# State-space set-up recast: paired complex products, blockwise powers, work moved to ScalarE and GpSimd

## The chip, the cores and the metric

The kernel runs on one core of one Trainium2 chip. The metric is the device time of one execution in microseconds (us); of the kernel before there are three timed runs, and the median counts.

## The reference, cut to what matters

One trunk layer is applied to two sequences of 1024 tokens (D_MODEL 1024) with the same weights: RMSNorm, one input projection, four token mixers (RG-LRU, gated linear attention, gated DeltaNet, S5), a gated merge, an output projection, a final norm. Two pieces matter here. DeltaNet's q, k and v go through a depthwise convolution of four taps and SiLU:

```python
qkv = jax.nn.silu(centred_dwconv(qkv.astype(f32), conv_w.astype(f32)))
```

S5 is a diagonal complex recurrence in 32 groups of 64 states, forward and reverse. Its parameters are made discrete from the weights alone:

```python
dt = jnp.exp(log_dt)[:, None]
mag = jnp.exp(lam_re * dt)
a_re, a_im = mag * jnp.cos(lam_im * dt), mag * jnp.sin(lam_im * dt)
...
bb_re = f_re[..., None] * b_re - f_im[..., None] * b_im
bb_im = f_re[..., None] * b_im + f_im[..., None] * b_re
...
s[t] = a * s[t-1] + bb @ u[t]        # complex, per group
y[t] = c_re @ s_re[t] - c_im @ s_im[t]
```

Nothing of the S5 set-up depends on the sequence.

## The kernel before, in words

The two sequences run one after the other (`for s in range(nseq)`), each in stages. A stage opens its own memory and PSUM banks and hands its generators to `weave`, which draws a step from whichever generator is least far along; this gives the order of the program. A framework scheduler with a simulated timeline then fixes the order of instructions on each engine, so work of a generator can move a little ahead or behind its place in the program. Engines run their own list in order. All operations go through small helpers, so the profile names line 54 for nearly all of them, and groups are told apart by tile names.

The stages of a sequence are, in order:

- **Projection stage.** `dn_proj` makes q, k, v and a gate for four heads, 16 steps. Each is one projection of 1024 x 128 in three-pass fp32r (`proj_steps`, 48 matmuls of 512 columns, weights split into `hi` on ScalarE and `lo` on GpSimd), evicted by ScalarE into `dup`. For q, k, v the convolution follows: one `tensor_scalar` for the first tap and three `scalar_tensor_tensor` for the others, all on VectorE (`conv`, tile `dcv`), then a sigmoid on ScalarE (`dsg`), a product on GpSimd, and, one step later, transposes on TensorE. Beside it run some blocks of the merge gate's projection (`early`, two of 48 matmuls in the first sequence, none in the second), and in the first sequence alone `s5_setup`, with 8 steps.
- **Recurrence stage.** `dn_core1` (triangular inverses of DeltaNet) and the RG-LRU blocks; in the first sequence also `s5_rot`, which builds a table of rotations for each of eight quads of groups and stores it (`rot_d`).
- **Attention and S5 stage**, then the merge and output stages. `s5_core` loads the stored tables.

`s5_setup` computes on 128 partitions (64 states x two directions). From small tiles of 128 x 32 (`s5t`) it makes the powers of a from 0 to 8 (`pw`), the rotations' seven squarings (`rot`), bb (`s5bb`), c transposed (`s5cc`) and re-ordered powers (`s5pwo`, 64 copies). Then each of eight quads of four groups forms two complex outer products on VectorE (`M` with `tq` as scratch, real and imaginary part each as two products and a sum), stores one (`tout_d`), transposes the other on TensorE (`Ti`, `tin_d`), copies the first shifted into `s5CA`, and multiplies bb with `s5CA` on TensorE into a bank where group g takes output partitions 32g to 32g+15; ScalarE evicts that into `Kt`, VectorE adds a diagonal (`dm`), and eight stores follow (`tk_d`). The matmul of that last step is:

```python
for ri in range(2):
    for g in range(4):
        mm(p[g * 32:g * 32 + 16, 0:240], bb[:, ri, qd * 4 + g],
           CA[:, ri, g].rearrange("p l i -> p (l i)"), start=(ri == 0), stop=(ri == 1))
```

All loads and stores of DRAM are issued by SyncE's queue in order.

## Time and profile before

| | |
|---|---|
| timed runs | 3162.29, 3163.14, 3171.67 us; median 3163.14 us |
| profiled execution, its own time | 3163.6 us |
| its span, first to last instruction | 3161.9 us (1.7 us around it) |
| mean granted TensorE clock | 0.961 of full speed |
| TensorE matmul, busy | 2884.7 us (91%), 15130 instructions |
| VectorE, busy | 1970.0 us (62%), 3909 instructions |
| ScalarE, busy | 1247.2 us (39%) |
| GpSimd, busy | 1075.7 us (34%) |

Busy time is the union of an engine's instructions, so overlapping matmuls are counted once. An average over the span mixes stages; the rows below therefore come from single stretches. A tile's row lists the instructions that read or write it. "Releaser" is what ended an engine's wait as the semaphores show it.

### The profile page before, as it was taken

How to read it: one execution, taken by the hardware profiler on the slowest of the kernel's cores; microseconds unless marked ns; L12 is line 12 of the kernel's file. 1: busy time of each engine (PE TensorE's matmuls, PEld its weight loads, DVE VectorE, ACT ScalarE, POOL GpSimd, SP SyncE). 2: the span in 40 equal slices, each digit the busy share in tenths (PEclk: the TensorE clock that was granted, in tenths of full speed). 3: DMA queues.
4: the chain of work that ended last, by engine and by line, in shares of the span. 5: the costliest groups of instructions: out<-in, count | busy, mean ns of one | idle time of the engine just before them, and what ended most of it. 6: DMA issues, size and time to landing. Idle time of an engine off the chain costs nothing. (4 is left out here: it accounts for less than half of the span.)

```text
span 3161.9 us, 41900 instructions
## 1 busy us (share of the span) xinstructions
PE 2884.7 (91%) x15130; PEld 2367.2 (75%) x15130; DVE 1970.0 (62%) x3909; ACT 1247.2 (39%) x1926; POOL 1075.7 (34%) x851
## 2 busy tenths in 40 slices
PE   6888779999996999999999988999999699999998
PEld 5666667778785788878778866777878588788877
DVE  6999786733658455665655367673366744557645
ACT  4333545543223334332354355653332334333223
POOL 2267552432343222111343333343324222221123
PEclk9999989999998999999999998999999899999999
DMA  5344535242242445563453342434224244565343
GB/s 105 98 125 149 177 102 159 80 150 67 87 142 89 142 138 185 195 203 121 162 186 103 102 135 83 154 89 138 67 90 142 86 142 127 188 207 193 117 150 124
DMA packets 430449, 418.97 MB, mean 133 GB/s; under 512 B 109953, under 2 KB 323489, under 8 KB 430241
## 3 DMA queue, kind: packets, MB, share of 16 engines
q1 hardware_dynamic: 430240, 416.29, 42.2%
q8 instruction: 119, 1.95, 0.3%
q14 instruction: 90, 0.73, 0.1%
HBM read 302.68 MB, written 113.51 MB: 132 GB/s over the span
## 5 line engine op out<-in xcount | busy, mean ns | idle before, releaser
L54 PE MATMUL pj<-xn,hi 128*128 128x512 f32 x4608 | 1481.0, 401 | 18.9 <-DVE misc L54 4.4
L54 POOL TENSOR_TENSOR lo<-raw,hi 128x512 fp32r<-128x512 f32 x432 | 614.0, 1425 | 1441.3 <-ACT hi L54 1333.2
L54 PEld LDWEIGHTS pj<-xn,hi 128*128 128x128 f32 x4608 | 871.6, 192 | 213.4 <-issue 11.7
L54 PE MATMUL pj<-xn,lo 128*128 128x512 f32 x2304 | 918.0, 398 | 0.0
L54 ACT CAST hi<-raw 128x512 fp32r<-128x512 f32 x432 | 265.1, 618 | 732.8 <-PE pj L54 498.7
L54 PEld LDWEIGHTS pj<-xn,lo 128*128 128x128 f32 x2304 | 441.9, 192 | 101.0 <-issue 7.9
L54 ACT ACT_TABLE_LOAD x194 | 248.9, 1283 | 140.6 <-DVE Ab L54 81.6
L54 PE MATMUL pj<-yh,hi 128*128 128x512 f32 x576 | 237.4, 412 | 3.2 <-DVE mg L54 3.2
L54 PE MATMUL pj<-yh,lo 128*128 128x512 f32 x576 | 226.1, 393 | 0.0
L54 PE MATMUL pj<-yl,hi 128*128 128x512 f32 x576 | 225.7, 392 | 0.2 <-DVE yl L54 0.2
L54 DVE TENSOR_TENSOR sg<-sg,pj 128x512 f32<-128x512 f32 x128 | 87.6, 685 | 97.3 <-PE pj L54 82.2
L54 PE MATMUL pj<-hi,mh 128*128 128x512 f32 x384 | 124.6, 401 | 6.4 <-ACT mh L54 4.1
L54 PEld LDWEIGHTS pj<-yh,lo 128*128 128x128 f32 x576 | 108.7, 189 | 23.8
L54 PEld LDWEIGHTS pj<-yh,hi 128*128 128x128 f32 x576 | 109.1, 189 | 22.3 <-DVE mg L54 4.0
L54 PEld LDWEIGHTS pj<-yl,hi 128*128 128x128 f32 x576 | 109.3, 190 | 18.9 <-DVE yl L54 0.5
L54 DVE TENSOR_TENSOR_SCAN w<-E,v 64x512 f32<-64x512 f32 x64 | 97.6, 1525 | 18.8 <-PE s L54 17.9
L54 ACT ACTIVATE fg<-pj,bmg 128x512 f32<-128x512 f32 x112 | 76.7, 686 | 69.8 <-issue 30.4
L54 DVE TENSOR_TENSOR yl<-yr,yh 128x512 fp32r<-128x512 f32 x80 | 59.5, 751 | 66.9 <-ACT yh L54 66.7
L54 POOL TENSOR_TENSOR v<-E,w 128x512 f32<-128x512 f32 x32 | 57.4, 1794 | 122.3 <-issue 71.2
L54 ACT ACTIVATE vn<-r,beta 128x128 f32<-128x128 f32 x128 | 40.5, 364 | 147.9 <-DVE vs L54 139.9
L54 DVE SCALAR_TENSOR_TENSOR dcv<-dup,dn_cw,dcv 128x1024 f32<-128x1024 f32 x72 | 96.8, 1344 | 1.3
L54 DVE TENSOR_TENSOR mg<-mg,sg 128x512 f32<-128x512 f32 x96 | 94.9, 989 | 2.1
(375 smaller groups left out, 4553.5 us busy)
## 6 DMA issues: line engine op xcount, KB each, us to landing
raw<-in_w_in_dram SPq DMA_DIRECT2D x176, 256.0 KB, 2.9
raw<-in_w_merge_gate_dram SPq DMA_DIRECT2D x128, 256.0 KB, 3.2
sl<-rows_d SPq DMA_DIRECT2D x128, 256.0 KB, 6.7
gs_d<-fg SPq DMA_DIRECT2D x112, 256.0 KB, 2.6
sg<-gs_d SPq DMA_DIRECT2D x112, 256.0 KB, 2.9
sl<-qkv_d SPq DMA_DIRECT2D x40, 512.0 KB, 4.6
raw<-in_w_branch_dram SPq DMA_DIRECT2D x64, 256.0 KB, 3.3
yr<-ysp SPq DMA_DIRECT2D x64, 256.0 KB, 3.2
```

The costliest lines, as they stand in the source:

```text
L54: i = f(*a, **kw)
```

## The change

It concerns the set-up of S5, and the first convolution tap of the first sequence.

- `conv` gets an argument: in the first sequence the first tap of DeltaNet's convolution is a scaled Copy on ScalarE instead of a VectorE `tensor_scalar` (12 of 1024 elements per partition). The second sequence keeps VectorE.
- Powers of a are made in three blocks (2; 3 and 4; 5 to 8) instead of seven steps, and a square takes 4 VectorE operations instead of 7.
- `s5bb` and `s5cc` each get a second, rotated copy (made on ScalarE), and `s5pwo` holds each power twice (16 ScalarE copies instead of 64 on VectorE). So each complex outer product is two products and one sum of 1024 elements per partition, instead of six operations of 512 and one sign change.
- `s5CA` and its copies are gone. The matmuls into `Kt` read `M` itself: per group three column ranges (112, 16 and 112 columns), each with its own weights (`b2` is bb with the other direction's half zero), real and imaginary part accumulated. The groups are now the outer loop. The diagonal is added by GpSimd.
- `s5_rot` does real and imaginary part in one operation, all of a quad on VectorE for even quads and on GpSimd for odd ones.
- `s5_setup` yields 32 times (8 while it loads c, 24 in the quads) instead of 8.

```diff
-    def conv(out, up, cw, bias=None):
-        if bias is None:
+    def conv(out, up, cw, bias=None, first=None):
+        if first is S:
+            act(out, up[:, 0:T], AF.Copy, scale=cw[:, 0:1])
+        elif bias is None:
             ts(V, out, up[:, 0:T], cw[:, 0:1], None, ALU.mult)
         else:
             ts(V, out, up[:, 0:T], cw[:, 0:1], bias, ALU.mult, ALU.add)
...
-            conv(cv, up, dn_cw[:, i * 4 + h])
+            conv(cv, up, dn_cw[:, i * 4 + h], first=S if s == 0 else V)
...
-    def cmul(ore, oim, are, aim, bre, bim, ta, tb, eng=V):
-        tt(eng, ta, are, bre, ALU.mult)
-        tt(eng, tb, aim, bim, ALU.mult)
-        tt(eng, tb, ta, tb, ALU.subtract)
-        tt(eng, ta, are, bim, ALU.mult)
-        tt(eng, oim, aim, bre, ALU.mult)
-        tt(eng, oim, oim, ta, ALU.add)
-        eng.tensor_copy(ore, tb)
+    def cmul(ore, oim, are, aim, bre, bim, ta, tb):
+
+        tt(V, ta, are, bre, ALU.mult)
+        tt(V, tb, aim, bim, ALU.mult)
+        tt(V, ore, ta, tb, ALU.subtract)
+        tt(V, ta, are, bim, ALU.mult)
+        tt(V, tb, aim, bre, ALU.mult)
+        tt(V, oim, ta, tb, ALU.add)
+
+    def csquare(ore, oim, re, im, ta, tb):
+        tt(V, ta, re, re, ALU.mult)
+        tt(V, tb, im, im, ALU.mult)
+        stt(oim, re, 2.0, im, ALU.mult, ALU.mult)
+        tt(V, ore, ta, tb, ALU.subtract)
...
+            eng = V if qd % 2 == 0 else G
...
-            for lv in range(7):
+            V.tensor_copy(E[:, 0:2, :, 1], rot[:, 0:3:2, 0, gs])
+            for lv in range(1, 7):
                 m = 1 << lv
-                b0, b1 = bc(rot[:, 0, lv, gs], m), bc(rot[:, 1, lv, gs], m)
-                e0, e1 = E[:, 0, :, 0:m], E[:, 1, :, 0:m]
-                f0, f1 = E[:, 0, :, m:2 * m], E[:, 1, :, m:2 * m]
-                tv = pl.tile([128, 4, 64], F32, tag="tm", name=nm("tm"))[:, :, 0:m]
-                tv2 = pl.tile([128, 4, 64], F32, tag="tm2", name=nm("tm2"))[:, :, 0:m]
...
-                tt(V, f0, e0, b0, ALU.mult)
-                tt(V, tv, e1, b1, ALU.mult)
-                tt(V, f0, f0, tv, ALU.subtract)
-                tt(G, f1, e0, b1, ALU.mult)
-                tt(G, tv2, e1, b0, ALU.mult)
-                tt(G, f1, f1, tv2, ALU.add)
+                both = [128, 2, 4, m]
+                e, f = E[:, 0:2, :, 0:m], E[:, 0:2, :, m:2 * m]
+                y = E[:, 2].rearrange("p a n -> p (a n)")[:, 0:8 * m].rearrange("p (r a n) -> p r a n", r=2, a=4)
+                tt(eng, f, e, bc(rot[:, 0, lv, gs].unsqueeze(1).to_broadcast([128, 2, 4]), m), ALU.mult)
+                tt(eng, y, e[:, ::-1], bc(rot[:, 1:3, lv, gs], m), ALU.mult)
+                tt(eng, f, f, y, ALU.add)
...
-        for e in range(2, 9):
-            cmul(pw[:, 0, e], pw[:, 1, e], pw[:, 0, e - 1], pw[:, 1, e - 1], pw[:, 0, 1], pw[:, 1, 1], ta, tb)
+        for e in (1, 2, 4):
+            n_ = [128, e, 32]
+            pa, pb = (pl.tile([128, 4, 32], F32, tag=x, name=nm(x))[:, 0:e] for x in ("pa", "pb"))
+            top = [pw[:, i, e].unsqueeze(1).to_broadcast(n_) for i in range(2)]
+            cmul(pw[:, 0, e + 1:2 * e + 1], pw[:, 1, e + 1:2 * e + 1], pw[:, 0, 1:e + 1], pw[:, 1, 1:e + 1], *top, pa, pb)
...
-        ts(V, tb[64:128], tb[64:128], -1.0, None, ALU.mult)
+        ts(V, sn[64:128], sn[64:128], -1.0, None, ALU.mult)
         tc_, td = t32(), t32()
-        for _ in range(3):
-            cmul(ta, tb, ta, tb, ta, tb, tc_, td)
-        V.tensor_copy(rr[:, 0], ta)
-        V.tensor_copy(ri[:, 0], tb)
+        csquare(tc_, td, cs, sn, ta, tb)
+        csquare(cs, sn, tc_, td, ta, tb)
+        csquare(rot[:, 0, 0], rot[:, 2, 0], cs, sn, ta, tb)
         for e in range(1, 7):
-            cmul(rr[:, e], ri[:, e], rr[:, e - 1], ri[:, e - 1], rr[:, e - 1], ri[:, e - 1], ta, tb)
+            csquare(rot[:, 0, e], rot[:, 2, e], rot[:, 0, e - 1], rot[:, 2, e - 1], ta, tb)
+        ts(V, rot[:, 1, 0:7], rot[:, 2, 0:7], -1.0, None, ALU.mult)
...
-            bb = ep.tile([128, 2, 32, 16], F32, name="s5bb")
-            braw = ep.tile([128, 2, 32, 16], F32, name="s5braw")
+
+            bb = ep.tile([128, 2, 32, 2, 16], F32, name="s5bb")
+            spare = ep.tile([128, 2, 2, 32, 16], F32, tag="b2", name="s5braw")
+            braw, tq = spare[:, 0], spare[:, 1, 0]
...
-                tt(V, bb[:, o], braw[:, x0], bc(fre, 16), ALU.mult)
+                b_ = bb[:, 0, :, o]
+                tt(V, b_, braw[:, x0], bc(fre, 16), ALU.mult)
                 tt(V, tq, braw[:, x1], bc(fim, 16), ALU.mult)
-                tt(V, bb[:, o], bb[:, o], tq, op)
-            cc = ep.tile([128, 2, 32, 16], F32, name="s5cc")
+                tt(V, b_, b_, tq, op)
+            act(bb[:, 1, :, 0], bb[:, 0, :, 1], AF.Copy, scale=-1.0)
+            S.copy(bb[:, 1, :, 1], bb[:, 0, :, 0])
+            cc = ep.tile([128, 2, 32, 2, 16], F32, name="s5cc")
             for i, nme in enumerate(("s5_c_re", "s5_c_im")):
...
+                    yield
                     transpose(p[:, b * 128:(b + 1) * 128], ld.rearrange("x d p -> x (d p)"), ident)
-                V.tensor_copy(cc[:, i].rearrange("p g i -> p (g i)"), p)
-
-            pwo = ep.tile([128, 2, 2, 32, 8], F32, name="s5pwo")
+                p3 = p.rearrange("p (g i) -> p g i", i=16)
+                if i == 0:
+                    S.copy(cc[:, 0, :, 0], p3)
+                    act(cc[:, 1, :, 1], p3, AF.Copy, scale=-1.0)
+                else:
+                    act(cc[:, 0, :, 1], p3, AF.Copy, scale=-1.0)
+                    S.copy(cc[:, 1, :, 0], cc[:, 0, :, 1])
+
+            b2 = ep.tile([128, 2, 32, 2, 16], F32, tag="b2", name="s5b2")
+            G.memset(b2, 0.0)
+            for d in range(2):
+                S.copy(b2[d * 64:d * 64 + 64, d], bb[d * 64:d * 64 + 64, 0])
+
+            pwo = ep.tile([128, 2, 2, 32, 2, 8], F32, name="s5pwo")
             for ri in range(2):
-                for t_ in range(8):
-                    V.tensor_copy(pwo[0:64, 0, ri, :, t_], pw[0:64, ri, 7 - t_])
-                    V.tensor_copy(pwo[64:128, 0, ri, :, t_], pw[64:128, ri, t_])
-                    V.tensor_copy(pwo[0:64, 1, ri, :, t_], pw[0:64, ri, t_ + 1])
-                    V.tensor_copy(pwo[64:128, 1, ri, :, t_], pw[64:128, ri, 8 - t_])
...
-            CA = ep.tile([128, 2, 4, 15, 16], F32, name="s5CA")
-            V.memset(CA, 0.0)
             for qd in range(NQ):
                 gs = slice(qd * 4, qd * 4 + 4)
                 prod = {}
-                for io, src in ((0, bb), (1, cc)):
-                    sh = [128, 4, 8, 16] if io else [128, 4, 16, 8]
-                    M = ep.tile(sh[:2] + [2] + sh[2:], F32, tag=f"M{io}", name=nm("M"))
-                    tq4 = ep.tile(sh, F32, tag=f"tq{io}", name=nm("tq4"))
-                    eng = V
-                    if io:
-                        P_ = lambda ri: bc(pwo[:, 1, ri, gs], 16)
-                        B_ = lambda ri: src[:, ri, gs].unsqueeze(2).to_broadcast(sh)
-                    else:
-                        P_ = lambda ri: pwo[:, 0, ri, gs].unsqueeze(2).to_broadcast(sh)
...
-                    tt(eng, M[:, :, 0], P_(0), B_(0), ALU.mult)
-                    tt(eng, tq4, P_(1), B_(1), ALU.mult)
-                    tt(eng, M[:, :, 0], M[:, :, 0], tq4, ALU.subtract)
-                    tt(eng, M[:, :, 1], P_(0), B_(1), ALU.mult)
-                    tt(eng, tq4, P_(1), B_(0), ALU.mult)
-                    tt(eng, M[:, :, 1], M[:, :, 1], tq4, ALU.add)
-                    if io == 1:
-                        ts(eng, M[:, :, 1], M[:, :, 1], -1.0, None, ALU.mult)
-                    prod[io] = M
+                for io, src in ((1, cc), (0, bb)):
+                    sh = [128, 8, 8, 16] if io else [128, 8, 16, 8]
+                    M = ep.tile(sh, F32, tag=f"M{io}", name=nm("M"))
+                    Y = ep.tile(sh, F32, tag="Y", name=nm("Y"))
+                    for o, i in ((M, 0), (Y, 1)):
+                        P_ = pwo[:, io, i, gs].rearrange("p g r t -> p (g r) t")
+                        B_ = src[:, i, gs].rearrange("p g r i -> p (g r) i")
+                        if io:
+                            P_, B_ = bc(P_, 16), B_.unsqueeze(2).to_broadcast(sh)
+                        else:
+                            P_, B_ = P_.unsqueeze(2).to_broadcast(sh), bc(B_, 8)
+                        tt(V, o, P_, B_, ALU.mult)
+                    tt(V, M, M, Y, ALU.add)
+                    prod[io] = M.rearrange("p (g r) a b -> p g r (a b)", r=2)
                 Mi, Mo = prod[0], prod[1]
-                dma(tout_d[qd], Mo.rearrange("p g r t i -> p g r (t i)"))
+                dma(tout_d[qd], Mo)
+                yield
...
-                        transpose(p[:, g * 128:(g + 1) * 128],
-                                     Mi[:, g, ri].rearrange("p j t -> p (j t)"), ident)
+                        transpose(p[:, g * 128:(g + 1) * 128], Mi[:, g, ri], ident)
...
-                for ri in range(2):
-                    V.tensor_copy(CA[0:64, ri, :, 8:15], Mo[0:64, :, ri, 0:7])
-                    V.tensor_copy(CA[64:128, ri, :, 0:7], Mo[64:128, :, ri, 1:8])
-                    ts(V, CA[:, ri, :, 7], cc[:, ri, gs], 1.0 if ri == 0 else -1.0, None, ALU.mult)
                 Kt = ep.tile([16, 4, 240], F32, tag="Kt", name=nm("Kt"))
+                yield
                 p = bank("st")
-                for ri in range(2):
-                    for g in range(4):
-                        mm(p[g * 32:g * 32 + 16, 0:240], bb[:, ri, qd * 4 + g],
-                           CA[:, ri, g].rearrange("p l i -> p (l i)"), start=(ri == 0), stop=(ri == 1))
+                for g in range(4):
+                    gg = qd * 4 + g
+                    for o, w, x in ((slice(0, 112), b2[:, 1], lambda ri: Mo[:, g, ri, 16:128]),
+                                    (slice(112, 128), bb[:, 0], lambda ri: cc[:, 0, gg, ri]),
+                                    (slice(128, 240), b2[:, 0], lambda ri: Mo[:, g, ri, 0:112])):
+                        for ri in range(2):
+                            mm(p[g * 32:g * 32 + 16, o], w[:, gg, ri], x(ri), start=(ri == 0), stop=(ri == 1))
...
-                tt(V, dm, ident[0:16, 0:16].unsqueeze(1).to_broadcast([16, 4, 16]), bc(dT[:, gs], 16), ALU.mult)
-                tt(V, Kt[:, :, 112:128], Kt[:, :, 112:128], dm, ALU.add)
+                tt(G, dm, ident[0:16, 0:16].unsqueeze(1).to_broadcast([16, 4, 16]), bc(dT[:, gs], 16), ALU.mult)
+                tt(G, Kt[:, :, 112:128], Kt[:, :, 112:128], dm, ALU.add)
...
-                    rot = bp.tile([128, 2, 8, 32], F32, name="rot")
-                    todo.append((8, s5_setup(pool("s5s", 1, stack=st), rot)))
+                    rot = bp.tile([128, 3, 8, 32], F32, name="rot")
+                    todo.append((32, s5_setup(pool("s5s", 1, stack=st), rot)))
```

## Rows read from the trace of the kernel before

**Rows 1.** Engines by stretch: PE, PEld, DVE, ACT, POOL busy us (count), PEclk, DMA, GB/s
```profile
49.30:337.80 288.50, 244.98 (x1174) 187.28 (x1175) 275.47 (x688) 109.42 (x186) 155.90 (x155) 0.95 0.38 122
1658.90:1846.70 187.80, 184.00 (x850) 149.02 (x849) 89.00 (x141) 83.80 (x126) 70.07 (x44) 1.00 0.33 101
337.80:743.30 405.50, 356.80 (x1933) 286.53 (x1932) 247.11 (x464) 201.65 (x278) 166.33 (x163) 0.94 0.41 125
1846.70:2240.70 394.00, 354.64 (x1910) 284.97 (x1910) 231.08 (x398) 199.49 (x273) 139.47 (x98) 0.93 0.39 118
```
**Rows 2.** First sequence, tiles that mark the projection stage's two ends: duration min/median/max, starts
```profile
L54 ACT COPY dup<-pj x24: 569/585/592, 49.3 to 312.7; 128x512 f32<-128x512 f32 x24
L529 SPq DMA_DIRECT2D rows_d<-rs x1: 737/737/737, 337.8 to 337.8; - x1
```
**Rows 3.** VectorE groups by shape, 60 to 340 us: busy us, mean ns | idle before
```profile
L54 DVE TENSOR_TENSOR M<-s5pwo,s5cc 128x512 f32<-128x512 f32 x16 | 19.6, 1252 | 0.0
L54 DVE COPY s5pwo<-pw 64x32 f32<-64x32 f32 x60 | 13.3, 226 | 0.7
L54 DVE TENSOR_TENSOR M<-s5pwo,s5bb 128x512 f32<-128x512 f32 x16 | 13.1, 840 | 0.0
L54 DVE TENSOR_SCALAR dcv<-dup,dn_cw 128x1024 f32<-128x1024 f32 x12 | 12.9, 1072 | 0.9 <-ACT dup L54 0.8
L54 DVE TENSOR_TENSOR s5t<-pw 128x32 f32<-128x32 f32 x21 | 7.2, 364 | 0.1
L54 DVE TENSOR_SCALAR M<-M 128x512 f32<-128x512 f32 x8 | 4.4, 548 | 0.0
```
**Rows 4.** Stretch, busy of tiles tq, dm, then E (DVE, POOL), E again (recurrence stage)
```profile
49.30:337.80 288.50, 49.93 (x64) 0.95 0.38 122
...
49.30:337.80 288.50, 7.35 (x15) 0.95 0.38 122
...
49.30:337.80 288.50, 32.18 (x108) 69.89 (x105) 0.95 0.38 122
...
337.80:743.30 405.50, 16.84 (x66) 28.11 (x63) 0.94 0.41 125
```
**Rows 5.** The same for tile s5CA: PE, PEld and DVE
```profile
49.30:337.80 288.50, 9.00 (x128) 2.47 (x128) 24.29 (x48) 0.95 0.38 122
```
**Rows 6.** Prices: VectorE product of 1024, ScalarE scaled pass of 1024, a weight load
```profile
L54 DVE TENSOR_TENSOR i<-i,r x16: 1201/1226/1803, 390.2 to 2151.8; 128x1024 f32<-128x1024 f32 x16
...
L54 ACT ACTIVATE a<-r,sp8n x16: 1147/1152/1157, 377.0 to 2139.8; 128x1024 f32<-128x1024 f32 x16
...
L54 PEld LDWEIGHTS st<-s5CA,s5bb x128: 92/95/97, 137.9 to 317.6; 128*16 128x16 f32 x128
```
**Rows 7.** Timeline of TensorE: start us, us, operation, count
```profile
203.16 0.60 PE L54 MATMUL st<-s5CA,s5bb 128*16 128x240 f32 x8 [1.44 <-DVE s5CA L54]
203.69 0.74 PE L54 MATMUL pj<-xn,hi 128*128 128x512 f32 x2
...
207.02 0.62 PE L54 MATMUL pj<-xn,hi 128*128 128x512 f32 x2
207.48 0.39 PE L54 MATMUL pj<-xn,lo 128*128 128x512 f32 x1
...
209.30 0.60 PE L54 MATMUL st<-ident,M 128*128 128x128 f32 x4
209.66 0.48 PE L54 MATMUL pj<-xn,hi 128*128 128x512 f32 x1
```
**Rows 8.** Timeline of GpSimd and VectorE over one collision
```profile
194.40 2.95 POOL L54 TENSOR_TENSOR dcv<-dcv,dsg 128x1024 f32<-128x1024 f32 x1
195.01 2.41 DVE L54 TENSOR_TENSOR dm<-ident,s5dT 16x64 f32<-16x64 f32 x1
```
**Rows 9.** Waits: us in total, times, longest; 40 to 335 us, then 330 to 480 us
```profile
ACT hi L54 <- DMA raw<-in_w_in_dram: 32.1, 7, 9.8
...
DVE E L54 <- DMA rot_d<-E: 7.7, 1, 7.7
```

More of the change, by code (lines that the diff above doesn't have):

```diff
@@ L1120, in s5_setup @@
                     dma(braw[d * 64:(d + 1) * 64, i], A[nme][0, d].rearrange("g p j -> p g j"))
-            tq = ep.tile([128, 32, 16], F32, name="s5tq")
             for o, (x0, x1, op) in ((0, (0, 1, ALU.subtract)), (1, (1, 0, ALU.add))):
-                tt(V, bb[:, o], braw[:, x0], bc(fre, 16), ALU.mult)
+                b_ = bb[:, 0, :, o]
+                tt(V, b_, braw[:, x0], bc(fre, 16), ALU.mult)
                 tt(V, tq, braw[:, x1], bc(fim, 16), ALU.mult)
-                tt(V, bb[:, o], bb[:, o], tq, op)
-            cc = ep.tile([128, 2, 32, 16], F32, name="s5cc")
+                tt(V, b_, b_, tq, op)
+            act(bb[:, 1, :, 0], bb[:, 0, :, 1], AF.Copy, scale=-1.0)
+            S.copy(bb[:, 1, :, 1], bb[:, 0, :, 0])
+            cc = ep.tile([128, 2, 32, 2, 16], F32, name="s5cc")
             for i, nme in enumerate(("s5_c_re", "s5_c_im")):
@@ L1132, in s5_setup @@
                         dma(ld[:, d], A[nme][0, d, b * 8:(b + 1) * 8].rearrange("g i p -> (g i) p"))
+                    yield
                     transpose(p[:, b * 128:(b + 1) * 128], ld.rearrange("x d p -> x (d p)"), ident)
-                V.tensor_copy(cc[:, i].rearrange("p g i -> p (g i)"), p)
-            pwo = ep.tile([128, 2, 2, 32, 8], F32, name="s5pwo")
-            for ri in range(2):
-                for t_ in range(8):
-                    V.tensor_copy(pwo[0:64, 0, ri, :, t_], pw[0:64, ri, 7 - t_])
-                    V.tensor_copy(pwo[64:128, 0, ri, :, t_], pw[64:128, ri, t_])
-                    V.tensor_copy(pwo[0:64, 1, ri, :, t_], pw[0:64, ri, t_ + 1])
-                    V.tensor_copy(pwo[64:128, 1, ri, :, t_], pw[64:128, ri, 8 - t_])
+                p3 = p.rearrange("p (g i) -> p g i", i=16)
[10 more added lines that the diff above has]
+            pwo = ep.tile([128, 2, 2, 32, 2, 8], F32, name="s5pwo")
+            for ri in range(2):
+                w = pw[:, ri].rearrange("p e g -> p g e")
+                for x in range(2):
+                    S.copy(pwo[0:64, 0, ri, :, x], w[0:64, :, 7::-1])
+                    S.copy(pwo[64:128, 0, ri, :, x], w[64:128, :, 0:8])
+                    S.copy(pwo[0:64, 1, ri, :, x], w[0:64, :, 1:9])
+                    S.copy(pwo[64:128, 1, ri, :, x], w[64:128, :, 8:0:-1])
             dT = ep.tile([16, 32], F32, name="s5dT")
             dma(dT, A["s5_d"][0].rearrange("(g j) -> j g", j=16))
-            CA = ep.tile([128, 2, 4, 15, 16], F32, name="s5CA")
-            V.memset(CA, 0.0)
             for qd in range(NQ):
@@ L1175, in s5_setup @@
                     for g in range(4):
-                        transpose(p[:, g * 128:(g + 1) * 128],
-                                     Mi[:, g, ri].rearrange("p j t -> p (j t)"), ident)
+                        transpose(p[:, g * 128:(g + 1) * 128], Mi[:, g, ri], ident)
                     S.copy(Ti[:, :, ri], p.rearrange("p (g n) -> p g n", g=4))
                 dma(tin_d[qd], Ti)
-                for ri in range(2):
-                    V.tensor_copy(CA[0:64, ri, :, 8:15], Mo[0:64, :, ri, 0:7])
-                    V.tensor_copy(CA[64:128, ri, :, 0:7], Mo[64:128, :, ri, 1:8])
-                    ts(V, CA[:, ri, :, 7], cc[:, ri, gs], 1.0 if ri == 0 else -1.0, None, ALU.mult)
                 Kt = ep.tile([16, 4, 240], F32, tag="Kt", name=nm("Kt"))
+                yield
                 p = bank("st")
-                for ri in range(2):
-                    for g in range(4):
-                        mm(p[g * 32:g * 32 + 16, 0:240], bb[:, ri, qd * 4 + g],
-                           CA[:, ri, g].rearrange("p l i -> p (l i)"), start=(ri == 0), stop=(ri == 1))
+                for g in range(4):
[5 more added lines that the diff above has]
+                            mm(p[g * 32:g * 32 + 16, o], w[:, gg, ri], x(ri), start=(ri == 0), stop=(ri == 1))
                 for g in range(4):
```

7 lines of the change are left out of this document (removed).

## The prediction, made from the kernel before alone

> **What bounds the kernel now.** The change touches the first sequence only, so I first looked for the same stage in both sequences and laid one beside the other, in the view of busy time by stretch. The stage's ends are read from two tiles: the first eviction of a projection into the convolution's input at 49.3 us and the store of the decay rows at 337.8 us [rows 2]; the second sequence's marks are the same instructions. In the first sequence the projection stage lasts 288.5 us, in the second 187.8 us [rows 1]. In the second TensorE is busy for 184.0 of 187.8 us at the full clock (2.4 GHz): it is the bound. In the first it is busy for 245.0 of 288.5 us at a mean of 0.95 of the clock, and it is VectorE that hardly pauses: 275.5 of 288.5 us, against 89.0 in the second sequence [rows 1]. The difference, 186.5 us, is the S5 set-up that runs beside. So in this one stage VectorE is the bound, and time taken from it comes back until TensorE's own work is the limit.
>
> How far away is that limit? A projection's matmul of 512 columns follows the one before it after 0.23 us (two in 0.46 us) [rows 7]. The stage holds everything that the second sequence's has (187.8 us), two more blocks of 48 matmuls (96 x 0.23 = 22.1 us), the transposes of the outer products (16 batches of four, 0.36 us from one batch's start to the next matmul, 5.8 us), some four such batches for c (1.4 us), and the matmuls into the convolution kernel: eight instructions per batch, 0.53 us to the next matmul [rows 7], 128 instructions [rows 5], so 16 batches, 8.5 us. That is 225.6 us of TensorE work in 288.5 us: 62.9 us are lost to waits and to the lower clock that goes with them.
>
> The recurrence stage offers nothing: it takes 405.5 us in the first sequence and 394.0 in the second [rows 1]; the first has one more block of the merge gate (48 x 0.23 = 11.0 us), which is all of the difference. The rotation tables that are built there cost no time now.
>
> **VectorE, part by part.** What leaves it altogether: the shifted copies, 24.3 us [rows 5]; the re-ordered powers, 13.3; the first tap, 12.9; the sign change, 4.4 [rows 3]; the diagonal, 7.4 [rows 4]. Sum 62.3 us. The outer products: the scratch tile's instructions are 49.9 us [rows 4] and the first products into M 19.6 and 13.1 [rows 3], together 82.6 us for 96 operations of 512. Afterwards there are 48 of 1024. At the price of an undisturbed product of that size, 1.226 us [rows 6], they cost 58.8 us; if each costs as much as the two it replaces, 82.6. I take the middle, 71: what stretches these instructions (their means are up to 1.25 us [rows 3]) is seen where GpSimd holds one: a VectorE sum of 64 elements takes 2.41 us and ends with GpSimd's product [rows 8]; and half as many can be held. Saved 12, between 0 and 24. Powers and squarings: 7 steps of 7 become 3 of 6, and 9 of 7 become 9 of 4, so 58 small operations fewer; at 0.226 to 0.364 us [rows 3] 13 to 21 us, and I take 15. The rotation tables: VectorE's part is 32.2 us in this stage and 16.8 in the next [rows 4], 49 for eight quads. It now does four quads with as many operations as before, each twice as long, so between 24 and 49 us, in either stage. In this stage it may lose 32 or gain 17; I take a gain of 9. VectorE is then left with 275.5 - 62.3 - 12 - 15 - 9 = 177 us, at least 135 and at most 217.
>
> **TensorE.** Its work grows. The new matmuls into Kt have 112, 16 and 112 columns, so as many columns as before, but the loop order is turned. Before, four groups stood one behind the other, each writing another strip of 32 output partitions, and the timeline shows what that gives: eight matmuls of 240 columns are over in 0.60 us [rows 7], where 512 columns of the same data type need as much to their end, so the strips work side by side. Now twelve instructions of one strip follow each other. Nothing in the trace shows small matmuls of one strip in a row; I bound them. Below: they overlap as today, 8.5 us. Above: the columns one after the other. There are 64 products, two passes each (128 records [rows 5]), of 240 columns, 30,720 columns. The transposes have the same data type: 512 columns take 0.36 us to the next matmul and 0.60 us to their end [rows 7], 0.70 or 1.17 ns a column, so 21.6 or 36 us. I take 24, near the step to the next matmul, since the matmuls behind don't wait for the last one's end. TensorE's work becomes 225.6 - 8.5 + 24 = 241 us. That is above VectorE's highest bound, so TensorE sets the stage.
>
> On top come waits. With none, as in the second sequence, the stage lasts 241 us; with all that are there now, 304, which would be a loss. I take 14 us, far nearer to the second sequence, since the same code without a full VectorE loses 3.8 us there; what is added is that the front of the stage still has a chain of small operations ahead of its first quad and that TensorE now meets transposes that wait for M. So 255 us, a gain of 33.5 us.
>
> **ScalarE, GpSimd, SyncE.** ScalarE takes 12 taps at 1.15 us [rows 6] = 13.8 us and 24 copies of at most 1024 elements, at most 27.6 us: at most 151 of 255 us with the 109.4 it has [rows 1]. The tap stands at the head of a chain that it leads on the same engine anyway (evict, tap, three VectorE taps, sigmoid), so it costs nothing as long as ScalarE isn't held; behind it are queued the next casts of weights. GpSimd loses the shared levels (69.9 us in this stage [rows 4]) and gets four whole quads, 56 to 112 us in either stage (14 us a quad now, twice the length then), and 16 small sums: at most 216 of 255. The number of DMAs is unchanged, and SyncE's queue carries the same stores; those of the last quad move from an eighth before the stage's end to its end, where eight stores stand ahead of the decay rows. I cost that at nothing, since the next stage opens with projections that need none of them; without that cover it costs a few microseconds, which the 14 us hold.
>
> The profiled execution took 3163.6 us, against a median of 3163.1, so the same sum holds for both: 3163.6 - 33.5 = 3130 us.
>
> **Rivals.** (1) The strips overlap after all, or waits vanish: the stage lasts 226 to 230 us, 3103 us. Against it: only the order of issue changed, and a strip has one set of weights at a time.
>
> (2) Weight loads come into the open. Each of the 384 new matmuls brings its own load of 95 ns [rows 6], as long as a matmul of 112 columns streams (79 ns). If none is hidden, 36.5 us more: 241 + 36.5 + 14 = 292 us, 3167 us, no change. Against it: eight such loads are issued with eight matmuls within 0.60 us, and the projections' loads hide behind 0.23 us [rows 7]. The Trainium skill, TensorE: Matmul & The Clock Gate, Part 3, says that a weight load overlaps matmuls in flight only where the row group differs; these all use the same rows, so by that rule this rival would be the case. The trace disagrees for the projections, whose loads use all rows too and hide; the same page lets a load into a background buffer go ahead.
>
> (3) The tap on ScalarE is held behind weight casts that wait for SyncE's loads: seven such waits, 32.1 us, up to 9.8 us each [rows 9]. If all of them pass on through the convolution to the transposes, the gain is gone: 3162 us. Against it: the sigmoid stands behind the same casts in the second sequence, and TensorE is full there.
>
> (4) Slower: the rotation table has one buffer. VectorE clears it for every quad and then must wait for GpSimd's whole quad and its store. Such a wait is there once now, 7.7 us [rows 9]. Behind it stand, in VectorE's order, the convolutions and evictions of either stage. Four GpSimd quads of 14 us give 56 us; if it all reached the path, 3130 + 56 = 3186 us. It decides from 43 us on. Against it: VectorE is idle for 158 us of the recurrence stage [rows 1], and the order is fixed with GpSimd's time in view.
>
> (5) VectorE stays the bound because GpSimd stretches it more than today; it would have to exceed its upper bound by a fifth. Then about 3140 to 3150 us.
>
> **How the numbers follow.** The forecast, with 3112 to 3150 around it, gets 0.68; (1) 0.05; (2) 0.08; (3) 0.08; (4) 0.08; (5) 0.03. About 0.3% (9.5 us) is what a measurement can tell from no change. Faster: 0.68 + 0.05 + 0.03 = 0.76; within: (2) and (3), 0.16; slower: (4), 0.08. The range runs from 3106, below which lies most of (1), to 3163, above which lie (4) and half of (2).
>
> **What would show it.** After the change the first sequence's projection stage should last about 255 us with TensorE busy in over 90% of it and VectorE in 150 to 200 us; a batch into Kt should take some 3 us per quad instead of two of 0.53; the recurrence stage should stay at 405 us within 5. Wrong would be: a stage of 280 us and more with VectorE idle; VectorE waits on the rotation table of tens of microseconds; a recurrence stage that is longer.

## The result, and the profile after

The changed kernel takes 3131.6 us (median of four, 3128.1 to 3137.0), the kernel before, timed beside it, 3162.7 us: a ratio of 0.9893 with a 95% interval of 0.9871 to 0.9915, so 31 us less; 3130 had been forecast. The profiled execution of the changed kernel takes 3133.5 us.

The busy time by stretch, first sequence, cut at the same marks as before: the projection stage, the recurrence stage, and the same two stretches for tile E (the rotation tables) alone. Columns as in [rows 1].

```profile
49.50:302.00 252.50, 240.62 (x1367) 194.38 (x1367) 170.63 (x292) 135.15 (x215) 101.65 (x65) 0.97 0.39 123
302.00:709.20 407.20, 364.02 (x1998) 292.29 (x1994) 262.25 (x497) 204.08 (x284) 190.68 (x197) 0.95 0.43 134
...
49.50:302.00 252.50, 0.00 (x0) 0.00 (x0) 0.97 0.39 123
302.00:709.20 407.20, 33.55 (x96) 54.10 (x96) 0.95 0.43 134
```

Beside [rows 1]: the projection stage is 36.0 us shorter (288.5 to 252.5); VectorE is busy for 171 of 252 us instead of 275 of 288, TensorE for 95% of the stage instead of 85%. The recurrence stage is 1.7 us longer, its start 0.2 us later, and everything behind it, whose code is the same, 4.0 us longer (2418.6 to 2422.6; over all profiles of this study this part lies between 2408 and 2423 us, so that is scatter). -36.0 + 1.7 + 0.2 + 4.0 = -30.1 us, the difference of the two profiled executions.

The last two lines show what was not forecast: against [rows 4], no rotation table at all is built in the projection stage now. Both engines do all of it in the recurrence stage. A table begins with two short operations on VectorE that set its first entries. The row of these operations, in the kernel before and then in the changed one (count, duration ns, first and last start us), and what the first one waits for in the changed kernel:

```profile
L54 DVE MEMSET E<- x16: 62/62/62, 3.8 to 431.0; 128x4 f32 x16
L54 DVE MEMSET E<- x16: 62/62/62, 311.3 to 515.3; 128x4 f32 x16
DVE E L54 <- DMA tk_d<-Kt: 8.0, 1, 8.0
```

In the kernel before the first table is begun at 3.8 us. In the changed one it is begun at 311.3 us, after a wait of 8.0 us for the last store of the last quad's `Kt`. Nothing in the arithmetic ties a table to `Kt`; in the program, memory that one pool gives back is taken by a later one, tile by tile (`reuse_waits`). So the tables now seem to lie in memory that the set-up uses to its end. That the set-up's new tile sizes moved them there is likely, and not shown.

VectorE's and ScalarE's groups in the projection stage of the changed kernel (busy us, mean ns | idle before, releaser), the new ones:

```profile
L54 DVE TENSOR_TENSOR M<-M,Y 128x1024 f32<-128x1024 f32 x16 | 26.9, 1684 | 0.4
L54 DVE TENSOR_TENSOR Y<-s5pwo,s5cc 128x1024 f32<-128x1024 f32 x8 | 13.8, 1726 | 0.2
L54 DVE TENSOR_TENSOR Y<-s5pwo,s5bb 128x1024 f32<-128x1024 f32 x8 | 13.1, 1634 | 0.2
L54 DVE TENSOR_TENSOR M<-s5pwo,s5cc 128x1024 f32<-128x1024 f32 x8 | 11.2, 1400 | 35.6 <-PE st L54 18.3 <-ACT s5cc L54 17.3
L54 DVE TENSOR_TENSOR M<-s5pwo,s5bb 128x1024 f32<-128x1024 f32 x8 | 10.5, 1318 | 18.2 <-PE st L54 18.2
...
L54 ACT COPY s5pwo<-pw 64x256 f32<-64x256 f32 x16 | 10.5, 658 | 3.3 <-DVE pw L54 3.1
```

The five product groups sum to 75.5 us (71 forecast). VectorE now waits: for TensorE's work that frees M (18.3 us for the matmuls into Kt, which read one product, and 18.2 us for the transposes of the other), and once for the transposed c (17.3 us, until ScalarE's copy `s5cc`). That copy follows the last transpose of c, which TensorE runs at 128.8 us in its order and without a pause before it; the loads for it were issued by 120.0 us and land 1.6 to 3.9 us later. In the kernel before, M's products hardly waited [rows 3]: the wait has changed sides.

TensorE's waits in the stage (us in total, times, longest), changed kernel:

```profile
PE pj L54 <- DVE dtk L54: 5.3, 1, 5.3
PE sm L54 <- DVE rw L54: 3.3, 1, 3.3
PE cr L54 <- DVE GG L54: 2.9, 1, 2.9
PE cr L54 <- DVE g L54: 0.4, 1, 0.4
```

That is 11.9 us, all of TensorE's idle time (252.5 - 240.6); before it was idle for 43.5.

The matmuls into Kt, TensorE's timeline over one batch (start us, us, operation):

```profile
186.33 0.61 PE L54 MATMUL pj<-xn,hi 128*128 128x512 f32 x2
186.88 0.56 PE L54 MATMUL st<-M,s5b 128*16 128x112 f32 x4
187.27 0.25 PE L54 MATMUL st<-s5cc,s5bb 128*16 128x16 f32 x4
187.37 0.56 PE L54 MATMUL st<-M,s5b 128*16 128x112 f32 x8
187.77 0.26 PE L54 MATMUL st<-s5cc,s5bb 128*16 128x16 f32 x4
187.88 0.56 PE L54 MATMUL st<-M,s5b 128*16 128x112 f32 x8
...
188.88 0.54 PE L54 MATMUL st<-M,s5b 128*16 128x112 f32 x4
189.36 0.50 PE L54 MATMUL pj<-xn,lo 128*128 128x512 f32 x1
```

A strip's twelve matmuls (three column ranges, real and imaginary part, two passes each) take 0.50 us from one strip's first 16-column matmul to the next's (187.27, 187.77, 188.28), so a quad's four strips take 2.0 us, and eight quads 16 us. In the kernel before two batches of eight took 1.06 us per quad [rows 7].

### The profile page after: what moved, and what is told of

It is laid out like the page before. It is cut to its first block, busy times and chain, and to the rows that moved or that the text cites. A ratio compares the mean times of both kernels' runs of the same rounds, so it can differ in the third digit from the quotient of the medians.

```text
span 3131.8 us, 42068 instructions
## 1 busy us (share of the span) xinstructions
PE 2891.2 (92%) x15386; PEld 2383.9 (76%) x15386; DVE 1880.0 (60%) x3569; ACT 1275.0 (41%) x1961; POOL 1043.8 (33%) x796
## 5 line engine op out<-in xcount | busy, mean ns | idle before, releaser
L54 POOL TENSOR_TENSOR lo<-raw,hi 128x512 fp32r<-128x512 f32 x432 | 605.9, 1406 | 1474.1 <-ACT hi L54 1371.6
L54 POOL TENSOR_TENSOR dcv<-dcv,dsg 128x1024 f32<-128x1024 f32 x24 | 60.3, 2512 | 145.4 <-ACT dsg L54 104.5
```

The costliest lines, as they stand in the source:

```text
L54: i = f(*a, **kw)
```

## The experiments

All stages in one table, each from its kernel's profile. "To the store" ends where the tables above end; "to rs" ends 0.4 to 4.1 us earlier, at ScalarE's copy of the decay rows. Expectations that give 252 or 288 us for the stage mean the first mark, those that give 250 the second. The ratio is to the kernel before on the same chip, with its interval; e6 and e7 were executed once, so their kernel times have no interval.

| kernel | stage to the store | to rs | TensorE busy | VectorE busy | recurrence | ratio |
|---|---|---|---|---|---|---|
| before | 288.5 | 287.6 | 245.0 | 275.5 | 405.5 | 1 |
| e1_tap_only | 285.6 | 284.6 | 247.1 | 263.2 | 409.3 | 0.9983 (0.9972 to 0.9995) |
| e5_finer_before | 291.5 | 290.7 | 242.8 | 270.2 | 404.6 | 1.0009 (0.9999 to 1.0019) |
| e10_rot_later | 268.8 | 267.4 | 239.3 | 244.8 | 412.4 | 0.9944 (0.9926 to 0.9961) |
| after | 252.5 | 249.7 | 240.6 | 170.6 | 407.2 | 0.9893 (0.9871 to 0.9915) |
| e2_tap_back | 253.9 | 249.8 | 240.5 | 183.0 | 405.4 | 0.9876 (0.9857 to 0.9896) |
| e8_rot_back | 252.1 | 249.4 | 239.9 | 171.0 | 412.1 | 0.9905 (0.9886 to 0.9924) |
| e3_strips | 241.9 | 238.8 | 228.0 | 175.9 | 411.4 | 0.9865 (0.9848 to 0.9881) |
| e4_pwo_vector | 247.8 | 245.1 | 238.8 | 182.7 | 406.0 | 0.9857 (0.9835 to 0.9879) |
| e9_best | 237.9 | 235.0 | 228.3 | 187.7 | 409.7 | 0.9871 (0.9853 to 0.9889) |
| e6_load2 | 259.4 | 257.2 | 238.0 | 216.1 | 413.0 | one execution: 3134.9 us |
| e7_load5 | 268.1 | 267.7 | 236.6 | 233.4 | 459.9 | one execution: 3186.9 us |

**The tap, from both sides.** First the kernel before with nothing but the first conv tap moved to ScalarE, then the changed kernel with the tap back on VectorE.

```diff
...
-            conv(cv, up, dn_cw[:, i * 4 + h])
+            conv(cv, up, dn_cw[:, i * 4 + h], first=S if s == 0 else V)
```

> The kernel before with one edit: the first convolution tap of the first sequence on ScalarE. Theory (VectorE is the bound of the first sequence's projection stage): the 12.9 us that leave VectorE come back in full, the stage falls from 288.5 to about 275 us and the kernel from 3163 to about 3150 us, VectorE still above 90% busy in the stage. Rival (the gain came from the finer interleaving of the set-up, or from the shorter chains, not from VectorE's time): the stage stays at 285 to 289 us, the kernel at 3160 us or more.

```diff
-            conv(cv, up, dn_cw[:, i * 4 + h], first=S if s == 0 else V)
+            conv(cv, up, dn_cw[:, i * 4 + h], first=V)
```

> The changed kernel with the first tap back on VectorE. Theory (VectorE is no longer the bound there, at 171 of 252 us): 13 us more on VectorE cost nothing; the stage stays within 4 us of 252 us and the kernel within 5 us of 3131. If ScalarE's queue is what still makes TensorE wait, it may gain 1 to 5 us. Rival (VectorE is still the limit): the stage grows by about 13 us, to 265.

The first was a miss: VectorE lost 12.3 us of work (275.5 to 263.2), the stage only 2.9, where 13 had been expected; stage and kernel (3160.4 us) came out where the rival had them, though not for its first reason (e5_finer_before below). VectorE's wait for the store of a table (us in total, times, longest), in the kernel before and then with the tap moved, where it is the longest of its waits:

```profile
DVE E L54 <- DMA rot_d<-E: 1.1, 1, 1.1
DVE E L54 <- DMA rot_d<-E: 11.3, 3, 4.3
```

The tables alone in its projection stage, busy time of VectorE and GpSimd:

```profile
49.40:335.00 285.60, 38.59 (x108) 67.56 (x105) 0.93 0.39 123
```

VectorE's idle time in the stage grows by 9.4 us (13.0 to 22.4), and the wait for the one table buffer by 10.2. So most of the time taken off VectorE came back as this wait. The same 108 table operations take 38.6 us instead of 32.2 [rows 4], but the rest of VectorE's work got shorter by nearly as much, so they don't account for it. In the second VectorE has 12.4 us more to do and neither the stage to rs nor the kernel is longer. So the tap's place is worth about 3 us of the stage before the other edits (the ratio's interval lies just below 1), and nothing that can be seen after them.

**The rotation tables alone.** The kernel before, with the first table held until the last small operation of the decay chain, so that they are built in the recurrence stage:

```diff
-    last_ln = []
+    last_ln, held = [], []
...
-        ts(V, ex[:, 0:2], ex[:, 0:2], -1.0, None, ALU.mult)
+        held[:] = [V.tensor_scalar(ex[:, 0:2], ex[:, 0:2], -1.0, None, ALU.mult)]
...
-            V.memset(E[:, 0, :, 0:1], 1.0)
+            i = V.memset(E[:, 0, :, 0:1], 1.0)
+            if qd == 0:
+                after(i, held[0])
```

> The kernel before with one edit: the first operation of the rotation tables on VectorE is held behind the last operation of the decay rows, so none of the tables is built in the projection stage (five of eight are now, with 32 us of VectorE and 70 us of GpSimd there). Nothing leaves VectorE in sum. Theory A (the tables that were pulled into the projection stage cost it their VectorE time, their stretching by GpSimd and waits on their stores, and the change gained by moving them out as well): the stage falls by 30 us or more, to 258 or less, and the recurrence stage grows by at most 10 us; the kernel at 3130 to 3145 us. Theory B (the tables only fill gaps in VectorE's order, and the recast products carry the gain): the stage falls by less than 12 us, and the kernel stays at 3150 us or more.

The projection stage and its tables, then the recurrence stage's tables:

```profile
49.70:318.50 268.80, 239.31 (x1171) 184.37 (x1172) 244.78 (x587) 109.10 (x185) 97.03 (x66) 0.97 0.38 119
...
49.70:318.50 268.80, 4.07 (x17) 6.44 (x16) 0.97 0.38 119
318.50:730.90 412.40, 58.68 (x159) 69.18 (x153) 0.93 0.42 130
```

Almost nothing but the place of the tables differs (a few operations that the hold doesn't reach still run early, and the first table starts 4.5 us before the stage's end), and the stage loses 19.7 us, where the whole change takes 36.0 off it. 6.9 us of it come back in the recurrence stage. The result lies between the two theories, 30 us or more and less than 12, and the kernel's 3146.9 us between their bounds too. So the tables' place is a large part of the gain and not all of it. No run has the recast products with the tables left where they were, so the other 16.3 us (268.8 to 252.5) belong to the rest of the change as a whole; what the products alone bring is not shown.

**What the yields do.** The set-up is a coroutine that the main work resumes; the change also cuts it finer. The kernel before, with three more yields and a larger share of steps:

```diff
...
-                    todo.append((8, s5_setup(pool("s5s", 1, stack=st), rot)))
+                    todo.append((32, s5_setup(pool("s5s", 1, stack=st), rot)))
```

> The kernel before with the changed kernel's finer steps alone: the set-up yields 32 times instead of 8. Theory (work on VectorE decides): the stage stays within 6 us of 288 us. Rival (the interleaving decides): the stage falls by 15 us or more without anything leaving VectorE.

Nothing gained (stage +3.0 us, ratio within 0.2% of 1), as expected.

**The order of the matmuls into Kt.** The changed kernel with the group loop innermost again:

```diff
-                for g in range(4):
-                    gg = qd * 4 + g
-                    for o, w, x in (...):
-                        for ri in range(2):
-                            mm(p[g * 32:g * 32 + 16, o], w[:, gg, ri], x(ri), start=(ri == 0), stop=(ri == 1))
+                for o, w, x in (...):
+                    for ri in range(2):
+                        for g in range(4):
+                            mm(p[g * 32:g * 32 + 16, o], w[:, qd * 4 + g, ri], x(g, ri), start=(ri == 0), stop=(ri == 1))
```

> The changed kernel with the matmuls into Kt in another order: the four groups, each with its own strip of 32 output partitions, are the inner loop again. Theory (matmuls of one strip run one after the other, 0.50 us per group now, and those of four strips side by side; TensorE is the bound of the stage): a quad's batch falls from 2.0 us to about 0.6, eight quads save 11 us, the stage falls from 252 to about 241 us and the kernel to about 3120. Rival (TensorE isn't the bound but waits on others for as long): the batches get shorter, the stage stays within 4 us of 252.

TensorE's timeline over one batch of it:

```profile
149.66 0.39 PE L54 MATMUL pj<-xn,hi 128*128 128x512 f32 x1
149.98 0.58 PE L54 MATMUL st<-M,s5b 128*16 128x112 f32 x16
150.37 0.28 PE L54 MATMUL st<-s5cc,s5bb 128*16 128x16 f32 x16
150.47 0.56 PE L54 MATMUL st<-M,s5b 128*16 128x112 f32 x16
150.97 0.50 PE L54 MATMUL pj<-xn,hi 128*128 128x512 f32 x1
```

The same 48 matmuls now start within 1.0 us instead of 2.0, where 0.6 had been expected, and the stage is 10.6 us shorter. That four strips written in turn work side by side was read from [rows 7]; here it is shown, though it halves the time and doesn't quarter it. Eight quads give 8 us of the 10.6; for the rest this run has no account. The kernel's 3125.5 us are above the expected 3120.

**ScalarE's copies.** The changed kernel with the 16 re-orderings of the product factors on VectorE:

```diff
-                    S.copy(pwo[0:64, 0, ri, :, x], w[0:64, :, 7::-1])
+                    V.tensor_copy(pwo[0:64, 0, ri, :, x], w[0:64, :, 7::-1])
...
```

> The changed kernel with the sixteen re-ordering copies of the powers on VectorE instead of ScalarE. Theory (these copies stand in one block of 10.5 us on ScalarE at 88 to 103 us, ahead of two evictions that TensorE needs; TensorE stands still for 5.7 us there and then runs at half the clock until 113 us): without the block the stage falls by 5 to 9 us, the kernel to about 3123 to 3127, and TensorE has no gap over 3 us between 85 and 115 us. Rival (the gap has another cause, such as loads held up in SyncE's queue): the gap stays and the stage is within 3 us of 252.

In the changed kernel, ScalarE's and then TensorE's timeline at that place (start us, us, operation [idle before, releaser]):

```profile
99.83 3.38 ACT L54 COPY s5pwo<-pw 64x256 f32<-64x256 f32 x5
103.22 2.10 ACT L54 COPY s5b<-s5bb 64x1024 f32<-64x1024 f32 x2
105.33 0.59 ACT L54 COPY dtk<-cr 128x512 f32<-128x512 f32 x1
105.92 1.28 ACT L54 ACT_TABLE_LOAD   x1
107.22 0.60 ACT L54 ACTIVATE dtk<-pj 128x512 f32<-128x512 f32 x1
...
108.59 1.22 PE L54 MATMUL pj<-xn,hi 128*128 128x512 f32 x2 [5.33 <-DVE dtk L54]
109.61 0.63 PE L54 MATMUL pj<-xn,lo 128*128 128x512 f32 x1
110.03 1.05 PE L54 MATMUL pj<-xn,hi 128*128 128x512 f32 x2
```

TensorE's next projection waits for a product of VectorE (dtk), and that for ScalarE's evictions dtk, which stand behind five re-orderings, two more copies and a table load of 1.3 us. TensorE idles for 5.3 us, and then runs at half the pace for some 4 us: one projection matmul per 0.43 us instead of 0.23, at a granted clock of 0.50 (1.2 GHz). With the copies on VectorE this gap is gone and the stage is 4.7 us shorter. But another wait, for VectorE's GG, grows from 2.9 to 5.45 us and ends at 94.1 us, so the expectation of no gap over 3 us between 85 and 115 us failed. Busy time by engine and granted clock of this stretch and the one before it, first the changed kernel:

```profile
74.75:100.00 25.25, 21.98 (x98) 17.54 (x97) 23.75 (x77) 17.53 (x27) 7.44 (x4) 0.93 0.20 57
100.00:125.25 25.25, 19.91 (x81) 16.08 (x80) 2.82 (x6) 15.88 (x23) 7.44 (x5) 0.86 0.42 130
```

The same two with the copies on VectorE:

```profile
75.15:100.40 25.25, 19.47 (x83) 15.52 (x82) 25.02 (x63) 15.56 (x22) 7.63 (x5) 0.86 0.25 77
100.40:125.65 25.25, 25.25 (x117) 20.64 (x116) 13.22 (x35) 9.47 (x15) 9.84 (x7) 1.00 0.39 116
```

The clock rises from 0.86 to 1.00 in the later stretch and falls from 0.93 to 0.86 in the earlier one. In both together TensorE works for 44.7 us instead of 41.9.

**How hard VectorE may be loaded.** The changed kernel with idle products of 1024 elements added to each of the 16 steps, two or five of them (32 and 80 in all, left unused):

```diff
                     tt(V, M, M, Y, ALU.add)
+                    for _ in range(2):
+                        tt(V, Y, M, M, ALU.mult)
```

> The changed kernel with 32 idle products of 1024 elements put on VectorE in the quads (two behind each outer product; they compute nothing that is used), 39 to 53 us. Theory (TensorE is the bound, VectorE at 171 of 250 us has room): VectorE comes to 210 to 224 us, the stage stays within 6 us of 250. Rival (VectorE is on the path through its latency): the stage grows by 20 us or more.

> The changed kernel with 80 idle products of 1024 elements on VectorE in the quads (five behind each outer product), 98 to 130 us. Theory: VectorE comes to 269 to 300 us, is full again and sets the stage, which then lasts 275 to 305 us, as before the change. Rival (TensorE's waits have another cause): the stage stays under 265 us.

With VectorE at 216 of 259 us the stage is 6.9 us longer, at 233 of 268 us 15.6: both between what theory and rival had given. TensorE's waits with two say how they are felt: it waits 5.5 us instead of 3.3 for a small VectorE result (rw), and 5.0 us for M and for Ti, for which it didn't wait before. With five, VectorE was expected to be full, at 269 us or more, and was not; the set-up no longer fits beside the projections. The stretch behind the stage's end, busy time by engine:

```profile
317.00:420.00 103.00, 63.20 (x371) 52.37 (x372) 87.28 (x150) 33.96 (x49) 29.38 (x36) 0.76 0.38 117
```

VectorE's costliest group in it, the added products (busy us, mean ns | idle):

```profile
L54 DVE TENSOR_TENSOR Y<-M 128x1024 f32<-128x1024 f32 x26 | 31.8, 1225 | 0.7
```

TensorE works for 63 of these 103 us at a granted clock of 0.76, and the recurrence stage is 53 us longer. So VectorE need not be full for its load to be felt, and what doesn't fit costs most in the next stage. The added products also stand in the set-up's own chain, ahead of the transposes, so these runs don't tell load from the longer chain.

**The form of the tables.** The changed kernel with the tables built as before (real parts on VectorE, imaginary parts on GpSimd):

```diff
-                tt(eng, f, e, bc(rot[:, 0, lv, gs].unsqueeze(1).to_broadcast([128, 2, 4]), m), ALU.mult)
-                tt(eng, y, e[:, ::-1], bc(rot[:, 1:3, lv, gs], m), ALU.mult)
-                tt(eng, f, f, y, ALU.add)
...
+                tt(V, f0, e0, b0, ALU.mult)
+                tt(V, tv, e1, b1, ALU.mult)
+                tt(V, f0, f0, tv, ALU.subtract)
+                tt(G, f1, e0, b1, ALU.mult)
+                tt(G, tv2, e1, b0, ALU.mult)
+                tt(G, f1, f1, tv2, ALU.add)
```

> The changed kernel with the rotation tables built as before: real parts on VectorE, imaginary parts on GpSimd, single products, for every quad; their place after the projection stage is not touched. Theory (the tables cost what they did only where they were built, in the projection stage; in the recurrence stage neither engine is short): VectorE spends some 45 to 55 us on them and GpSimd 90 to 110 in the recurrence stage, against 34 and 54, and neither stage moves: 250 and 407 to 412 us, kernel 3128 to 3135 us. Rival (the quads built whole on one engine are what made the tables cheap, or what costs the recurrence stage its 2 to 4 us): the recurrence stage moves by 5 us or more, up with the work or down with the whole quads gone.

```profile
302.00:714.10 412.10, 69.30 (x176) 76.10 (x168) 0.95 0.43 132
```

The tables cost VectorE 69.3 us instead of 33.6 and GpSimd 76.1 instead of 54.1. 45 to 55 and 90 to 110 us had been expected. The first stage doesn't move; the recurrence stage is 4.9 us longer in this profile, just under the bound that the rival was given, and the ratios of the two kernels can't be told apart. e10_rot_later, with the old form in the same place, has the same 412 us, but e3_strips and e6_load2, with the new form, have 411 and 413. So whether the form is worth some 5 us is not settled.

**Both repairs.** Group loop innermost and copies on VectorE:

> The changed kernel with both repairs at once: the group loop innermost in the matmuls into Kt, and the 16 re-orderings of the outer products' factors on VectorE. Theory (TensorE's own work sets the first projection stage, and the two repairs remove two different things, the 16 us of matmuls of one strip in a row and the gap at 108 us): the gains add, 11 and 4.6 us, so the stage is about 250 - 15.5 = 234 us, and VectorE, with some 9 us more work, stays under 190 us. Of the 15 us, 3 to 5 come back in the recurrence stage as they did with the strips alone. Kernel about 3116 us, ratio to the kernel before 0.984 to 0.986. Rival (VectorE is near its limit again or the freed time meets the same waits for the loads of c): the gains don't add, the stage stays at 238 to 241 us and the kernel at 3121 to 3126 us.

```profile
48.80:286.70 237.90, 228.25 (x1398) 183.13 (x1401) 187.71 (x310) 124.50 (x199) 103.72 (x65) 0.98 0.42 130
```

In the stage the gains add: 252.5 - 237.9 = 14.6 us, against 10.6 + 4.7. TensorE is busy for 96% of it. The kernel missed its mark: 3116 us and a ratio of at most 0.986 had been expected, the rival had 3121 to 3126. It takes 3119.5 us, 40.8 less than the kernel before on its chip, where the changed kernel had 31.1 less; but the intervals of the two ratios overlap, and of e3_strips, e4_pwo_vector and e9_best none can be told from the others by the kernel's time. What the stage shows is sure, what the kernel keeps of it is not.

## Why the prediction was right

**The bound: right for the kernel after, too simple for the one before.** After the change TensorE's own work sets the stage: putting 12.4 us back on VectorE (e2_tap_back) costs nothing, taking 8 us off TensorE (e3_strips) brings 10.6. Before it VectorE was in the way, but the step "time taken from it comes back until TensorE's own work is the limit" failed where it was tried alone: 12.3 us less on VectorE brought 2.9 us (e1_tap_only), because VectorE then waited for the one table buffer, which the sum of its work left out.

**VectorE after: 177 us forecast, 170.6 measured, by luck: two errors cancel.** The step on the rotation tables failed: a gain of 9 us with a range up to 32 was taken, and the whole 32.2 left, with GpSimd's 69.9. In the changed kernel the first table waits for the last quad, until 311 us, which no line of the diff says. e10_rot_later shows that this move alone, priced in the forecast as a side effect, takes 19.7 us off the stage of the kernel before, over half of the 36.0. The other terms came out too high: 62.3 + 12 + 15 = 89.3 us forecast, 275.5 - 170.6 - 32.2 = 72.7 measured. The reason is in how durations were added, for group by group they were about right. The groups of the kernel before add up to 313.4 us in a stage in which VectorE is busy for 275.5, those of the changed kernel to 187.6 for 170.6. That is 125.8 us less, of which 33.5 are the tables' and 92.3 the other terms', against 89.3 forecast. But neighbouring records overlap: by 37.9 us before, 55 ns for each of 688 instructions, and by 17.0 us now, 58 ns for each of 292. The 20.9 us between the two never were VectorE's time.

**The batches: 24 us forecast, 16 measured** (2.0 us per quad, where 3 had been named). The bounds were 8.5 and 36; a strip's twelve matmuls at 0.50 us are 480 columns in two passes, 960 in all, 0.52 ns a column, cheaper than the transposes' step of 0.70 that the value was taken from.

**The waits: 14 us forecast, about 19 measured.** TensorE's work, 225.6 - 8.5 + 16 = 233.1, leaves 19.4 of 252.5 us: 11.9 idle, the rest at a clock of 0.97. So 24 + 14 = 38 stands against 35.4, and 255 us against 252.5: again two errors of opposite sign. The kernel's time is nearer still by luck: the stage gained 2.5 us more than forecast, and the rest of the kernel is 5.9 us longer in the profile, 4.0 of it scatter. 5 of the 19 us go with ScalarE (e4_pwo_vector), whose work the sum put at nothing: that was argued for the tap, where it holds, and not for the re-orderings, which stand ahead of an eviction.

**What VectorE's load costs: mis-sized.** The sum took it that VectorE up to 217 us would not be felt. e6_load2, at 216, has 6.9 us more. In the changed kernel with more and more work on VectorE the stage takes 252.5, 253.9, 259.4 and 268.1 us with VectorE at 171, 183, 216 and 233 us (and 247.8 us at 183 where that work is ScalarE's copies). Over all kernels busy time alone doesn't give the stage: e5_finer_before has 291.5 us at 270, the kernel before 288.5 at 275.

**The recurrence stage: right** (407.2, within 5 of 405). Some of its 1.7 us is the last batch into Kt, whose last matmul starts at 303.7 us, behind the mark. That tables built there cost no time is not shown: with the old form and all tables there (e10_rot_later) the stage is 6.9 us longer than in the kernel before.

**The rivals.** (1) No: the batches do get longer; but with the order put back and the copies moved the stage comes to 238 us. (2) No: twelve matmuls with twelve loads start within 0.50 us, where the loads alone would be 12 x 0.095 = 1.14 us one after the other. The loads of the changed kernel, all of them and then eight of the batch shown above, whose eight matmuls start at 187.37 us (start us, us):

```profile
L54 PEld LDWEIGHTS st<-M,s5b x256: 92/95/150, 151.1 to 303.6; 128*16 128x16 f32 x128
187.35 0.33 PEld L54 LDWEIGHTS st<-M,s5b 128*16 128x16 f32 x8
```

Eight loads of 95 ns lie within 0.33 us, so their records overlap one another, and they run while the eight matmuls do. The Trainium skill, TensorE: Matmul & The Clock Gate, Part 3, has a load overlap matmuls in flight only where the row group differs. All of these use the same rows, so the measurement speaks against that rule here, as does the whole stage: loads are busy for 194.4 and matmuls for 240.6 of its 252.5 us. (3) Not behind the casts, but the mechanism has a relative: the re-orderings of e4_pwo_vector. (4) No: VectorE doesn't wait for GpSimd's store. GpSimd waits for VectorE's tables instead, 30.8 us in the recurrence stage, and TensorE has no wait on a table. (5) No: VectorE's share fell to 68%, although its products of 1024 did cost 75.5 us and not 71.

## What to carry to other kernels

When a full engine bounds one stage, first look for work on it that no one in that stage needs: building the rotation tables one stage later, alone, took 19.7 us off a stage from which the whole rewriting took 36.0, and brought about half of the kernel's gain (ratio 0.9944 against 0.9893). Look also where a table's memory lies: it can decide when the table is built. Price what leaves a full engine by its busy time, not by the sum of its records, and before taking an engine with idle time for free, read what stands behind the new work in its queue. A loop order that looks neutral on paper can double the time of small matmuls: let neighbouring ones write different strips.

## What the runs showed of the hardware

Matmuls of one strip of 32 output partitions in a row follow each other at 0.50 us per twelve (480 columns in two passes); in turn over four strips the same work takes half as long. Their weight loads, 95 ns each, show no time of their own: eight lie within 0.33 us beside eight matmuls. VectorE's records overlap by 55 ns each in this stage (37.9 us in 688 instructions), so a group of small operations is worth less than its durations say. A ScalarE re-ordering of 64x256 elements takes 658 ns, with little between the shortest and the longest (634 and 672), though half of them read in reverse. One pause of 5.3 us on TensorE was followed by some 4 us at half pace, a granted clock of 0.50 (1.2 GHz); a shorter one, of 2.9 us up to 90.1 us, was also followed by matmuls every 0.43 us for some 3 us.
